# Sample states of a hybrid decoder step: values fetched two steps ahead instead of one

## The chip, the core and the metric

The kernel runs on one core of one Trainium2 chip. The metric is the device time of one execution in microseconds (us); before the change its median is 1824.19 us over three runs.

The engines have these names in the profile: PE is TensorE's matmul, PEld its weight load, DVE is VectorE, ACT is ScalarE, POOL is GpSimd, SP is SyncE. Each engine works through its own queue in order. SP, ACT and POOL also issue DMAs from their queues.

## The reference

One layer of a decoder trunk runs for a prompt of 256 tokens and for 8 samples of one token each. The width is 2048. A combined input projection feeds three parallel mixers: a gated MLP over chunks, HGRN2 (8 heads, 128 x 128 states) and GLA (4 heads, 128 x 256 states). Each mixer's output is projected, gated and summed; an output projection, a residual and a squared-ReLU MLP of width 8192 follow. All weights are float32.

The part that the change touches is the recurrence of the samples. Each sample brings a state per head, and makes one step:

```python
S_t = diag(f_t) S_{t-1} + k_t v_t^T      # per head, dk x dv
o_t = S_t^T q_t
```

The new states are outputs (`hgrn_sample`, `gla_sample`), and `o_t`, normalised per head, goes on into the branch.

## The kernel before

**Matmuls.** Every weight block comes by DMA into a raw buffer (SP's queue, L606 and L613), ACT rounds it into `whi` (L109), DVE takes the rest into `wlo` (L106), and TensorE multiplies three times (L656 to L658): high by high, high by low, low by high. One such block of four 128-row slices by 256 columns is a *granule* of 24 matmuls. Raw buffers and the split tiles `whi` and `wlo` are few, so ACT and DVE run only some granules ahead of TensorE, and SP can load only when a split has emptied a buffer.

**Background work.** After each granule `linear` calls `background()` (L698). It raises the count `now`, pumps two queues of generators, and decides on a *slot*. `bg` holds the mixers of the prompt, `bs` the states of the samples. A queue gains its rate (0.5 per granule for `bs`) and spends 1 at each plain `yield`. A generator that yields a condition is held, without cost, until the condition is true; while held it saves up at most 1. The slot (L665) issues small matmuls for prompt levels (L678) and for samples (L685) that are at least 2 granules old. It comes when a round of the conditioning matrix (`ada`, L376) is due and something waits, or when something has waited for four granules (a GLA sample counts two more).

**Sample states.** `samples_r` (L1066) runs once for each of three groups: HGRN2 heads 0 to 3, HGRN2 heads 4 to 7, and GLA. A step handles one sample for HGRN2 (4 heads, 8 steps) and half a sample for GLA (2 heads, 16 steps). Each step does this:

- `fetch` brings the old states into a tile `st` (L1081), of which there are `ST_BUFS = 4`.
- `values` brings the row of v, broadcast to all partitions, from a DRAM scratch `vs_d` into a tile `vbc` (L1087), of which there are `VB_BUFS = 2`.
- ACT scales the states by the decay (L1107), DVE adds the product of k and v (L1109).
- The new states are stored (L1110), and a whole sample is handed to the slot, whose matmuls (L685) read the same `st` tile. DVE collects their results in `os` (L692, L694).

All four DMAs are issued from POOL's queue. Before step n's computation the generator fetches the states of step n+2 and the values of step n+1. The fetch is held until at most one computed tile is still waiting for its slot (L1100), and the computation until its states were fetched 3 granules ago and its values 2 (L1104).

**What orders the work.** From L972 to L1404 the orders on TensorE and POOL are those of the program text, as written. The orders on ACT, DVE and SP are made by the scheduler, which places each instruction by its own estimate of when the data are there. On the chip an instruction that comes too early in its queue holds up all that stands behind it.

**Who needs the results.** `finish(i)` (L1300) needs the finished `os` of a group: TensorE transposes it (L1307). It is called for both HGRN2 groups at the head of branch 1 and for GLA at the head of branch 2.

**Tiles touched by the change.** `os0`, `os1`, `os2` are three rows of results (128, 128 and 256 columns); the tag `os2` serves again after the output projection as `sp` (L1504). `A1` (L469) holds the scales of the first modulation, `A2` (L1494) those of the second; `G1` (L1407) and `G2` (L1603) hold the gates of the two residuals. Each of these four takes 576 bytes of a partition.

Of the kernel before, what the change touches and what calls it, by code (L numbers as in the profile page):

```python
# [15 lines left out]
P = 128  # L16
D = 2048
KT = D // P
# [3 lines left out]
NC = 1 + NS  # L22
# [13 lines left out]
CHUNKS = (2, 2, 4, 4, 4)  # L36
RATES = ((1.8, 0.5), (1.6, 0.5), (1.25, 0.5), (1.0, 0.5))
ST_BUFS = 4
VB_BUFS = 2
N_PRE = 6  # L40
PRE_AT = (2, 3, 4)
ADA_BATCH = 4
# [15 lines left out]
def hybrid_step_kernel(  # L58
# [8 lines left out]
    nc = tc.nc  # L67
# [14 lines left out]
    def nm(s):  # L82
        uid[0] += 1
        return f"{s}_{uid[0]}"

    def blk(shape=None, dt=F32):
        shape = shape or [P, 4, NT]
        return blkp.tile(shape, dt, tag="b", name=nm("b"))
# [4 lines left out]
    def tmp(shape, tag, bufs=2):  # L93
        return tp.tile(shape, F32, tag=tag, name=nm(tag), bufs=bufs)

    def const(shape, name, dt=F32):
        return cp.tile(shape, dt, tag=name, name=name)

    def mul(o, a, b):
        V.tensor_tensor(o, a, b, op=ALU.mult)  # L100
# [106 lines left out]
    def rstd_small(ms, scale, out):  # L207

        n, w = out.shape
        xx, aa = tmp([P, 16], "sx")[0:n, 0:w], tmp([P, 16], "sa")[0:n, 0:w]  # L210
        c = 0
        for m in ms if isinstance(ms, list) else [ms]:
            V.tensor_scalar(xx[:, c:c + m.shape[1]], m, scale, EPS, ALU.mult, ALU.add)
            c += m.shape[1]
        V.tensor_scalar(out.bitcast(I32), xx.bitcast(I32), -0.5, 1597463007.0, ALU.mult, ALU.add)
        for _ in range(3):
            mul(aa, out, out)
            V.scalar_tensor_tensor(aa, aa, -0.5, xx, ALU.mult, ALU.mult)
            V.scalar_tensor_tensor(out, aa, 1.5, out, ALU.add, ALU.mult)
# [249 lines left out]
    A1 = const([P, KT, NC], "A1")  # L469
# [254 lines left out]
    def tiles(bl):  # L724
        return lambda k: moving(bl[k // 4][:, k % 4, :])
# [123 lines left out]
    def to_tokens(vt):  # L849

        ps = sm()
        for m in range(2):
            for t in range(2):
                T.transpose(ps[:, (2 * m + t) * P:(2 * m + t + 1) * P], vt[:, m, t * P:(t + 1) * P], ident)  # L854
        return ps.rearrange("p (m t f) -> p t m f", m=2, t=2)
# [176 lines left out]
    def gla_group():  # L1032
# [30 lines left out]
        G.gates = gates  # L1063
        return G

    def samples_r(G):  # L1066

        dv = G.dv
        nj, nh = dv // P, 512 // dv
        q, k, g = G.q, G.k, G.g  # L1070
        fs = tmp([P, 4, NS], "fs")
        S.activation(fs, g[:, :, NP:NT], AF.Exp)
        qm = blk([P, 4, NS, 32])
        mul(qm, q[:, :, NP:NT].unsqueeze(3).to_broadcast([P, 4, NS, 32]),
            delta.rearrange("p (b c) -> p b c", b=NS).unsqueeze(1).to_broadcast([P, 4, NS, 32]))
        steps = [(b, h) for b in range(NS) for h in range(0, 4, nh)]
        ahead, vals = [], []

        def fetch(b, h):
            st = tmp([P, nh, dv], "st", ST_BUFS)  # L1080
            nc.gpsimd.dma_start(st, G.s_in(b, h, nh))  # L1081
            ahead.append((st, now[0]))

        def values(b, h):
            v = tmp([P, 4, P], "vbc", VB_BUFS)
            r0 = 4 * nj * b + h * nj
            nc.gpsimd.dma_start(v, vs_d[G.i, r0:r0 + 4, :].partition_broadcast(P))  # L1087
            vals.append((v.rearrange("p (h j) v -> p h (j v)", h=nh), now[0]))

        for s in steps[0:2]:  # L1090
            fetch(*s)
            yield
        values(*steps[0])
        yield
        os_ = tmp([P, dv], f"os{G.i}", 1)
        sts = []
        for n, (b, h0) in enumerate(steps):
            if n + 2 < len(steps):

                yield lambda: len(sts) + sum(len(x[3]) for x in samples) <= ST_BUFS - 3  # L1100
                fetch(*steps[n + 2])
            if n + 1 < len(steps):
                values(*steps[n + 1])
            yield lambda: now[0] >= max(ahead[0][1] + FETCHED, vals[0][1] + FETCHED - 1)  # L1104
            st, v = ahead.pop(0)[0], vals.pop(0)[0]
            for i in range(nh):
                S.activation(st[:, i, :], st[:, i, :], AF.Copy, scale=fs[:, h0 + i, b:b + 1])  # L1107
            for i in range(nh):
                V.scalar_tensor_tensor(st[:, i, :], v[:, i, :], k[:, h0 + i, NP + b:NP + b + 1], st[:, i, :], ALU.mult, ALU.add)  # L1109
            nc.gpsimd.dma_start(G.s_out(b, h0, nh), st)  # L1110
            sts.append(st)
            if h0 + nh == 4:
                samples.append((now[0], (G, qm, os_), b, sts))
                sts = []
            yield
        yield lambda: not samples
        yield READY
        ss, rr = tmp([P, 1], "sss", 1), tmp([P, 1], "srr", 1)
        S.activation(tmp([P, dv], "vt"), os_, AF.Square, accum_out=ss)
        rstd_small(ss, 1.0 / dv, rr)  # L1120
        S.activation(os_, os_, AF.Copy, scale=rr)
        G.os = os_
        yield

    def mixer_r(G):
# [18 lines left out]
        q, k, g = G.q, G.k, G.g  # L1144

        bs.g.append(samples_r(G))


# [258 lines left out]
    G1 = const([P, KT, NC], "G1")  # L1407
# [8 lines left out]
    def gated(m, src, Gv):  # L1416

        k = 2 * m
        sq = tmp([P, 2, NT], "vt")
        g = tmp([P, 2, NT], "gt")  # L1420
        if m < 7:
            S.activation(sq, src, AF.Square)
        else:
            S.activation(sq[:, 0, :], src[:, 0, :], AF.Square)
        V.tensor_scalar(g[:, 1, 0:NP], src[:, 1, 0:NP], Gv[:, k + 1, 0:1], None, ALU.mult)
        if m == 7:
            S.activation(sq[:, 1, :], src[:, 1, :], AF.Square)
        S.activation(g[:, 0, 0:NP], src[:, 0, 0:NP], AF.Copy, scale=Gv[:, k, 0:1])
        if m == 0:
            add(sqacc, sq[:, 0, :], sq[:, 1, :])  # L1430
        else:
            add(sqacc, sqacc, sq[:, 0, :])
            add(sqacc, sqacc, sq[:, 1, :])
        mul(gs[:, k:k + 2, :], src[:, :, NP:NT], Gv[:, k:k + 2, 1:NC])
        return g
# [13 lines left out]
    def put_rows(m, pt, rows):  # L1449
        S.copy(in_rows(rows, 0, m), pt[:, 0])  # L1450
        V.tensor_copy(in_rows(rows, 1, m), pt[:, 1])
# [28 lines left out]
    for m in range(8):  # L1480
        if m in PRE_AT:
            n = N_PRE // len(PRE_AT)
# [8 lines left out]
            S.activation(tmp([P, 1], "srr", 1), sqacc[:, 0:1], AF.Sqrt)  # L1491
    rounds.drain()
    rounds = pre
    A2 = const([P, KT, NC], "A2")  # L1494
    V.scalar_tensor_tensor(A2, mod[:, 4 * KT:5 * KT, :], 1.0, gpre2T.unsqueeze(2).to_broadcast([P, KT, NC]), ALU.add, ALU.mult)
    B2 = mod[:, 3 * KT:4 * KT, :]
    order.__exit__(None, None, None)
# [36 lines left out]
    Q.tensor_tensor(xsT, xsT, gs, op=ALU.add)  # L1534
    Q.tensor_tensor(xa, xsT, A2[:, :, 1:NC], op=ALU.mult)

# [50 lines left out]
    def put_quad(q, i2, i, src, vt):  # L1587
        k = 4 * q + 2 * i2 + i
        if i == 0 and (q == 0 or i2 == 0):
            V.tensor_scalar(vt[:, i, 0:NP], src, A2[:, k, 0:1], B2[:, k, 0:1], ALU.mult, ALU.add)  # L1590
        else:
            S.activation(vt[:, i, 0:NP], src, AF.Identity, scale=A2[:, k, 0:1], bias=B2[:, k, 0:1])
        if q == 0 or i == 1:
# [6 lines left out]

    rate[:] = (0.0, 0.0)
    rounds.pace, rounds.batch = 5, 2
    G2 = const([P, KT, NC], "G2")  # L1603
    h2H, h2L = tiles(h2h), tiles(h2l)

    def begin_up():
# [33 lines left out]
    def down(f, ah, al):  # L1640
        for m in range(8):
# [8 lines left out]
            if f == NFB - 1:  # L1650
                g = gated(m, dst, G2)
                later.append((now[0], lambda m=m, g=g: put_rows(m, to_tokens(g), yt)))
# [6 lines left out]
    for f in range(NFB):  # L1659
        nxt = up(f + 1) if f + 1 < NFB else None  # L1660
        if f == NFB - 1:
            rounds.drain()
            mul(G2, mod[:, 5 * KT:6 * KT, :], gpost2T.unsqueeze(2).to_broadcast([P, KT, NC]))
            yt = [[blk([P, 1024]) for _ in range(2)] for _ in range(2)]
# [23 lines left out]
    def last_tile(i):  # L1688
# [10 lines left out]
        S.activation(sq[:, i, :], d, AF.Square)  # L1699
        V.tensor_scalar(g[:, i, 0:NP], d[:, 0:NP], G2[:, 14 + i, 0:1], None, ALU.mult)  # L1700

# [43 lines left out]

    Q.tensor_tensor(gs[:, 14:16, :], dst[:, :, NP:NT], G2[:, 14:16, 1:NC], op=ALU.mult)  # L1746
    ys = tmp([P, NS, KT], "sqs", 1)
# [61 lines left out]
```

## Time and profile before

| | us |
|---|---|
| median of 3 runs (lowest to highest) | 1824.19 (1822.34 to 1824.85) |
| the profiled execution | 1821.87 |
| its span, first to last instruction | 1820.0 |

| engine | busy us | share of the span |
|---|---|---|
| TensorE | 1780.2 | 98% |
| VectorE | 1178.7 | 65% |
| ScalarE | 996.9 | 55% |
| GpSimd | 136.9 | 8% |

The profile is of one execution. The page lists busy time by engine and by line; other views ask the same trace for the waits (an engine and line, what it waited for, total us, number of times, longest), for stretches of the span, or for the order of time. In the order of time a row has its start, its duration, the engine, the line, the operation, the tiles written and read, and in brackets how long the engine sat idle before it and what ended that. Durations and waits that matter here are quoted with the prediction. GpSimd's DMA rows are only the issue of the transfer; the time to landing is in a table of its own.

### The profile page before, as it was taken

The numbers are of one execution on the slowest core, as the hardware profiler recorded it, in microseconds if no ns is written. First come the engines' busy times: TensorE is split into PE (matmuls) and PEld (weight loads), VectorE is DVE, ScalarE is ACT, GpSimd is POOL, SyncE is SP. The second block draws the span as 40 slices with busy tenths as digits, with TensorE's granted clock in tenths as the row PEclk, the third lists the DMA queues.
The fourth block names the chain that finished last, engine by engine and source line by source line (L and its number), as shares of the span: only waits on it lengthen the run. The fifth ranks groups of instructions, "written<-read, shape, count | busy, mean of one in ns | idle before, by whom it ended". The sixth has DMA issues, their size and how long they took to land.

```text
span 1820.0 us, 42083 instructions
## 1 busy us (share of the span) xinstructions
PE 1780.2 (98%) x16970; PEld 1689.8 (93%) x16970; DVE 1178.7 (65%) x2077; ACT 996.9 (55%) x1824; POOL 136.9 (8%) x228
## 2 busy tenths in 40 slices
PE   6999999999999999999999999999999999999998
PEld 4889999989988989989999989999999999999998
DVE  4666567787577696566555667555666666666666
ACT  5444364676766766654445666555554545454544
POOL 3221000102111111210000000000000000000000
PEclk9999999999999999999999999999999999999999
DMA  9987788788788789897978954777666666666663
GB/s 325 339 348 262 253 282 261 211 257 290 231 290 264 227 271 301 274 321 243 307 248 267 330 168 152 251 256 223 195 196 194 195 196 196 197 196 193 196 193 118
DMA packets 330180, 442.05 MB, mean 243 GB/s; under 512 B 14947, under 2 KB 276945, under 8 KB 329985
## 3 DMA queue, kind: packets, MB, share of 16 engines
q1 hardware_dynamic: 311872, 380.52, 65.1%
q0 software_dynamic: 17184, 57.85, 9.0%
q8 instruction: 133, 2.18, 0.5%
q10 hardware_dynamic: 928, 0.99, 0.2%
q14 instruction: 63, 0.51, 0.1%
HBM read 427.60 MB, written 11.70 MB: 241 GB/s over the span
## 4 chain that ended last, share of the span: by engine, by line
PE 88%; DVE 2%; issue 2%; DMA 1%; ACT 1%; POOL 0%; ACTq 0%; DVEq 0%; POOLq 0%
PE mm L656 27%; PE mm L658 26%; PE mm L657 26%; PE ada L376 3%; DMA vbc<-vs_d 1%; PE ada L308 1%; PE sm L854 1%; DVE wlo L106 1%; PE sm L678 1%; PE sm L685 0%; DVE b L106 0%; PE sm L1578 0%; PE sm L1209 0%; DMA st<-in_state_hgrn_dram 0%; ACT whi L109 0%
## 5 line engine op out<-in xcount | busy, mean ns | idle before, releaser
L656 PE MATMUL mm<-b,whi 128*128 128x264 f32 x4608 | 1286.9, 279 | 6.8 <-ACT whi L109 2.5
L658 PE MATMUL mm<-b,wlo 128*128 128x264 f32 x4608 | 1274.5, 277 | 5.2 <-DVE wlo L106 4.8
L657 PE MATMUL mm<-b,whi 128*128 128x264 f32 x4608 | 1273.4, 276 | 0.5 <-DVE b L106 0.4
L106 DVE TENSOR_TENSOR wlo<-raw,whi 128x512 fp32r<-128x512 f32 x1136 | 768.8, 689 | 443.8 <-ACT whi L109 442.4
L109 ACT CAST whi<-raw 128x512 fp32r<-128x512 f32 x1136 | 688.9, 616 | 626.9 <-DVE wlo L106 310.7
L656 PEld LDWEIGHTS mm<-b,whi 128*128 128x128 f32 x4608 | 872.3, 189 | 48.7 <-issue 26.4
L658 PEld LDWEIGHTS mm<-b,wlo 128*128 128x128 f32 x4608 | 872.3, 189 | 7.1 <-DVE wlo L106 7.1
L657 PEld LDWEIGHTS mm<-b,whi 128*128 128x128 f32 x4608 | 872.4, 189 | 1.1 <-DVE b L106 0.6
L103 DVE TENSOR_TENSOR b<-b,mm 128x528 f32<-128x528 f32 (+1 forms) x137 | 95.4, 698 | 63.3 <-PE mm L658 55.6
L1109 DVE SCALAR_TENSOR_TENSOR st<-vbc,b,st 128x128 f32<-128x128 f32 (+1 forms) x96 | 34.2, 392 | 52.4 <-DMA vbc<-vs_d 45.9
L1107 ACT ACTIVATE st<-st,fs 128x128 f32<-128x128 f32 (+1 forms) x96 | 37.0, 430 | 48.2 <-DMA st<-in_state_hgrn_dram 28.2
L1746 POOL TENSOR_TENSOR gs<-b,G 128x16 f32<-128x16 f32 x1 | 0.2, 222 | 714.1 <-DVE b L103 714.1
L485 POOL DMA_DIRECT2D b<-in_w_ada_dram x64 | 46.3, 725 | 48.0 <-PE ada L308 30.4
L376 PE MATMUL ada<-araw,cT 128*32 128x512 f32 x296 | 40.7, 601 | 0.0
L308 PE MATMUL ada<-b,cT 128*32 128x256 f32 (+1 forms) x640 | 35.0, 355 | 5.3 <-DMA b<-in_w_ada_dram 5.3
L100 DVE TENSOR_TENSOR b<-b,b 128x512 f32<-128x512 f32 (+1 forms) x47 | 34.0, 743 | 1.3 <-ACT b L1221 1.0
L308 PEld LDWEIGHTS ada<-b,cT 128*32 128x32 f32 x640 | 17.8, 113 | 17.4 <-DMA b<-in_w_ada_dram 9.6
L1110 POOL DMA_DIRECT2D out_dram<-st x32 | 23.5, 735 | 129.5 <-DVE st L1109 129.5
L376 PE MATMUL ada<-b,cT 128*32 128x512 f32 x216 | 26.2, 593 | 0.0
L106 DVE TENSOR_TENSOR b<-gt,b 128x528 fp32r<-128x528 f32 x32 | 22.7, 711 | 3.2
L106 DVE TENSOR_TENSOR b<-b,b 128x1056 fp32r<-128x1056 f32 (+3 forms) x21 | 20.9, 993 | 5.9 <-ACT b L109 5.9
L106 DVE TENSOR_TENSOR b<-b 128x1024 f32<-128x1024 f32 (+1 forms) x24 | 24.3, 1018 | 0.0
(360 smaller groups left out, 895.8 us busy)
## 6 DMA issues: line engine op xcount, KB each, us to landing
raw<-in_w_in_dram SPq DMA_DIRECT2D x231, 512.0 KB, 5.0
raw<-in_w_mlp_up_dram SPq DMA_DIRECT2D x128, 512.0 KB, 3.9
raw<-in_w_mlp_down_dram SPq DMA_DIRECT2D x128, 512.0 KB, 3.7
araw<-in_w_ada_dram SPq DMA_DIRECT2D x74, 512.0 KB, 5.7
b<-in_w_ada_dram SPq DMA_DIRECT2D x54, 512.0 KB, 6.4
b<-in_w_ada_dram POOLq DMA_DIRECT2D x48, 512.0 KB, 11.3
raw<-in_w_branch_dram SPq DMA_DIRECT2D x48, 512.0 KB, 4.6
raw<-in_w_out_dram SPq DMA_DIRECT2D x32, 512.0 KB, 5.1
```

Of the source, the lines that this page charges most:

```text
L100: V.tensor_tensor(o, a, b, op=ALU.mult)
L103: V.tensor_tensor(o, a, b, op=ALU.add)
L106: V.tensor_tensor(o, a, b, op=ALU.subtract)
L109: S.copy(hi, src)
L308: T.matmul(acc[32 * j:32 * j + 32, 0:n], cT[:, k, :], w[:, n * j:n * j + n], start=k == 0, stop=k == KT - 1)
L376: T.matmul(self.acc[32 * j:32 * j + 32, :], cT[:, k, :], ws[j // 2][:, j % 2 * 512:j % 2 * 512 + 512], start=k == 0, stop=k == KT - 1)
L485: queue.dma_start(w[:, i], w1[k * P:(k + 1) * P, :, self.k0 * P:(self.k0 + self.n) * P])
L656: T.matmul(o, a, xh(k + j), start=first and j == 0, stop=False)
L657: T.matmul(o, a, xl(k + j), start=False, stop=False)
L658: T.matmul(o, b, xh(k + j), start=False, stop=last and j == n - 1)
L1107: S.activation(st[:, i, :], st[:, i, :], AF.Copy, scale=fs[:, h0 + i, b:b + 1])
L1109: V.scalar_tensor_tensor(st[:, i, :], v[:, i, :], k[:, h0 + i, NP + b:NP + b + 1], st[:, i, :], ALU.mult, ALU.add)
```

## The change

Three things change in `samples_r`. The values of the first two steps are asked for before the loop, with one more `yield`. In the loop, the values of step n+2 are asked for first, then the store of the step before is issued, and then, behind the held condition, the states of step n+2 are fetched; a step's own store is only put aside, and the last one is issued after the loop. `vbc` has three buffers.

Room for the third buffer (2 KB of each partition) comes from tiles: the two HGRN2 groups share one row of results with the tag `os2`, which GLA then takes anew, `A2` is the tile of `A1`, and `G2` that of `G1`.

```diff
-VB_BUFS = 2
+VB_BUFS = 3
...
+    os_rows = []
+
     def samples_r(G):
...
         for s in steps[0:2]:
             fetch(*s)
             yield
-        values(*steps[0])
-        yield
-        os_ = tmp([P, dv], f"os{G.i}", 1)
-        sts = []
+        for s in steps[0:2]:
+            values(*s)
+            yield
+        if G.i != 1:
+            os_rows.append(tmp([P, 256], "os2", 1))
+        os_ = os_rows[-1][:, G.i % 2 * P:G.i % 2 * P + dv]
+        sts, out = [], []
         for n, (b, h0) in enumerate(steps):
             if n + 2 < len(steps):
+                values(*steps[n + 2])
+            if out:
+                nc.gpsimd.dma_start(*out.pop())
+            if n + 2 < len(steps):
 
                 yield lambda: len(sts) + sum(len(x[3]) for x in samples) <= ST_BUFS - 3
                 fetch(*steps[n + 2])
-            if n + 1 < len(steps):
-                values(*steps[n + 1])
             yield lambda: now[0] >= max(ahead[0][1] + FETCHED, vals[0][1] + FETCHED - 1)
...
-            nc.gpsimd.dma_start(G.s_out(b, h0, nh), st)
+            out.append((G.s_out(b, h0, nh), st))
             sts.append(st)
...
             yield
+        nc.gpsimd.dma_start(*out.pop())
         yield lambda: not samples
...
-    A2 = const([P, KT, NC], "A2")
+    A2 = A1
...
-    G2 = const([P, KT, NC], "G2")
+    G2 = G1
```

## The prediction, before the change was run

> **What bounds the kernel now.** I read the page first, then stretches of the span, then the waits by stage, then the order of time at two places. The page has TensorE busy for nearly the whole span, so a change can only win what TensorE idles, or what it loses to a lower clock.
>
> ```profile
> PE 1780.2 (98%) x16970; PEld 1689.8 (93%) x16970; DVE 1178.7 (65%) x2077; ACT 996.9 (55%) x1824; POOL 136.9 (8%) x228
> ```
>
> The table of stretches (length, then busy time and instructions of PE, PEld, DVE, ACT, POOL, then clock, DMA share, GB/s) says where that idle time lies.
>
> ```profile
> 350.00:500.00 150.00, 147.22 (x1650) 137.02 (x1649) 109.72 (x211) 110.64 (x225) 21.97 (x34) 0.99 0.79 252
> 500.00:630.00 130.00, 126.89 (x1489) 117.74 (x1489) 91.02 (x183) 87.23 (x191) 13.74 (x20) 1.00 0.81 264
> 630.00:810.00 180.00, 174.97 (x1852) 162.28 (x1852) 125.64 (x220) 107.55 (x218) 34.55 (x52) 0.99 0.87 290
> 1120.00:1800.00 680.00, 680.00 (x6036) 672.19 (x6035) 423.32 (x646) 352.55 (x585) 0.00 (x0) 1.00 0.67 203
> ```
>
> The first three are the stretches in which the samples' states of the three groups are done (two HGRN2 groups, then GLA). TensorE idles 2.78, 3.11 and 5.03 us in them, 10.9 us together. The last row, the MLP, idles nothing and no edit reaches into it. The waits of TensorE alone, in the same three stretches, name the stalls (total, times, longest):
>
> ```profile
> PE mm L656 <- ACT whi L109: 1.8, 1, 1.8
> PE mm L658 <- DVE wlo L106: 1.0, 2, 0.6
> ...
> PE mm L656 <- ACT att L1187: 1.3, 1, 1.3
> PE mm L658 <- DVE wlo L106: 0.8, 2, 0.4
> PE sm L678 <- issue: 0.6, 1, 0.6
> ...
> PE mm L658 <- DVE wlo L106: 2.8, 1, 2.8
> PE sm L678 <- issue: 2.2, 1, 2.2
> ```
>
> TensorE is stopped by weights that ACT and DVE have not split yet. These two run their queues in order, and the waits of the whole span say what holds them up:
>
> ```profile
> DVE st L1109 <- DMA vbc<-vs_d: 45.9, 18, 7.2
> ACT st L1107 <- DMA st<-in_state_hgrn_dram: 28.2, 9, 8.9
> ACT st L1107 <- DMA st<-in_state_gla_dram: 13.7, 8, 2.8
> ```
>
> Behind a waiting L1109 on DVE stand splits (L106), and for the splits wait TensorE and the loads into the raw buffers. The change aims at the first row. The second and third rows, the states themselves, are the same kind of wait on ACT.
>
> **The order on the GpSimd queue.** Write F(n) for the fetch of step n's states (L1081), V(n) for its values (L1087), C(n) for its two computations (L1107, L1109), S(n) for the store (L1110). Before, the queue reads F(n+1), V(n), S(n-1), F(n+2), V(n+1), S(n). After, it reads F(n+1), V(n+2), S(n-1), F(n+2), V(n+3), S(n). So V(n+2) stands where V(n) stood, and all F and S keep their order. V(n+2) needs the buffer that C(n-1) read last, of three; the store S(n-1) behind it waits for the same C(n-1). The new wait on GpSimd therefore holds nobody longer than the store did: F(n+2) and what follows are issued as before. Cost 0; the store's wait is the cover, and without it the cost would be one DVE group, 0.9 us (the 0.88 us of L1109 in the next rows). Numbers of instructions and DMAs are unchanged: 32 of each kind.
>
> **What it is worth, place by place.** First the end of the GLA group:
>
> ```profile
> 782.21 0.72 POOL L1081 DMA_DIRECT2D st<-in_state_gla_dram  x1
> 788.41 0.71 POOL L1110 DMA_DIRECT2D out_dram<-st  x1 [4.91 <-DVE st L1109]
> 789.12 0.58 POOL L1087 DMA_DIRECT2D vbc<-vs_d  x1
> 789.69 0.51 ACT L1107 ACTIVATE st<-st,fs 128x256 f32<-128x256 f32 x1
> 795.95 0.88 DVE L1109 SCALAR_TENSOR_TENSOR st<-vbc,b,st 128x256 f32<-128x256 f32 x2 [4.25 <-issue]
> 796.74 4.38 DVE L106 TENSOR_TENSOR wlo<-raw,whi 128x512 fp32r<-128x512 f32 x7
> ```
>
> The last values went out at 789.12, only after the store of step 13, though the states of step 15 had been fetched at 782.21 and scaled at 789.69. DVE stood 4.25 us for them with seven splits queued behind; TensorE ran dry and lost the 2.78 us of the waits above. After the change V(15) goes out before S(12) and F(15), so it is there before its states: DVE's 4.25 us exceed TensorE's 2.78 us, and I take the whole stall away. A stall this long also costs clock:
>
> ```profile
> 398.00:400.00 2.00, 1.56 (x8) 1.50 (x8) 1.97 (x5) 2.00 (x4) 0.00 (x0) 0.56 0.19 26
> 400.00:402.00 2.00, 2.00 (x12) 2.00 (x12) 2.00 (x4) 1.65 (x4) 0.00 (x0) 0.59 1.01 328
> 674.00:676.00 2.00, 2.00 (x21) 2.00 (x20) 2.00 (x6) 1.88 (x4) 0.00 (x0) 1.00 0.93 312
> 798.00:800.00 2.00, 2.00 (x11) 2.00 (x11) 2.00 (x5) 1.02 (x3) 0.00 (x0) 0.50 0.75 194
> 800.00:802.00 2.00, 2.00 (x16) 1.85 (x19) 1.19 (x3) 0.58 (x2) 0.00 (x0) 0.75 1.01 302
> ```
>
> From 798 to 802 us the clock was 0.50 and 0.75: (0.50 + 0.25) x 2 us = 1.5 us of work lost. So the end is worth **2.8 + 1.5 = 4.3 us** (bounds 0 and 4.3). The Trainium skill ("TensorE: Matmul & The Clock Gate", Part 1: The HAM clock gate) says that after an idle window of about 3.4 us the clock halves, and needs as long of work to return. By that rule, 1.7 us a stall, the end is worth 4.5 us. The trace agrees here (0.50), but shows that not each stall pays: after the one of 2.2 us at 672 us the clock was 1.00 in the next row.
>
> Second, the starts of the two HGRN2 groups. The first:
>
> ```profile
> 388.30 0.76 POOL L1110 DMA_DIRECT2D out_dram<-st  x1 [28.22 <-DVE st L1109]
> 389.05 0.75 POOL L1081 DMA_DIRECT2D st<-in_state_hgrn_dram  x1
> 389.80 0.55 POOL L1087 DMA_DIRECT2D vbc<-vs_d  x1
> 396.03 0.98 ACT L1107 ACTIVATE st<-st,fs 128x128 f32<-128x128 f32 x3 [8.91 <-DMA st<-in_state_hgrn_dram]
> 396.97 0.88 DVE L1109 SCALAR_TENSOR_TENSOR st<-vbc,b,st 128x128 f32<-128x128 f32 x3 [6.11 <-DMA vbc<-vs_d]
> ```
>
> S(0) released F(3) and V(2) one after the other. V(2) goes out at the start of the group after the change, but F(3) still stands behind S(0), and ACT still waits for it: the wait moves from the values to the states, 0.94 us earlier at most (396.97 less 396.03). TensorE lost 1.75 + 0.43 us here, the 1.8 by ACT and part of the 1.0 by DVE, and (0.44 + 0.41) x 2 = 1.7 us of clock, which on the 1.56 us busy of the first row makes 1.5. I take the DVE part, **0.4 us** (bounds 0 and 2.2 + 1.5 = 3.7). The second group's start is of the same kind with 0.8 us of DVE splits in the waits: I take **0.8 us** (0 to 0.8). The remaining stalls, 1.3 us by ACT's `att` and 2.8 us of "issue", have no value transfer as releaser: 0 (bounds 0 and 4.1).
>
> Third, the many short waits in between: DVE will now follow L1107 directly, so what it saves is the time by which values landed after states. TensorE did not stop there; 0.
>
> **The other parts.** The extra yield in front of each group shifts C(0) by two granules (a granule is one background call, 24 matmuls, about 680 us x 24 / 6036 = 2.7 us in the MLP's row). With two steps' values in hand the gate on values never holds, and both steps of a GLA sample come in one granule. Counting the pump's rules by hand, the last slot comes at granule 53 instead of 49 for the first group, at 93 for the second as before, at 142 instead of 148 for GLA. The outputs are asked for at 98, 98 and 162, so nobody waits: 0. If the second group slipped past 98, TensorE would wait for L1119 to L1121, some 4 us by these rows, which is no part of my sum:
>
> ```profile
> 616.66 0.31 ACT L1119 ACTIVATE vt<-os 128x128 f32<-128x128 f32 x1
> 620.09 0.40 ACT L1121 ACTIVATE os<-os,srr 128x128 f32<-128x128 f32 x1 [0.85 <-DVE srr L219]
> ```
>
> The shared tiles add only write-after-read waits. `A2` over `A1` waits for the modulation, over since the input projection; `G2` over `G1` waits for the last gated tile of the output projection, six MLP blocks earlier; the GLA row over the HGRN2 row waits for transposes that stand three granules ahead of that group's start. All are long past: 0, and if one were not, one small DVE operation late, below the 0.9 us named. The GpSimd queue also carries the prompt states' stores (L1254); their place among the samples' entries shifts by a step at most, which I price at 0.
>
> **Sum**, against the profiled execution (1821.87 us, span 1820.0): 4.3 + 0.4 + 0.8 = 5.5 us, so 1816.4 us. That execution lies 2.3 us below the median 1824.19 of the runs shown, so on the median's scale **1818.7 us**.
>
> **Rivals.**
>
> *The wait only changes its transfer.* ACT's 28.2 + 13.7 us for states stay, DVE follows ACT, and the last steps stop on F(14) and F(15) as they stopped on V(15). For it: F(n) keeps its place, and the two kinds land alike (rows below). Against it: F(15) had landed by 789.69, six us before V(15). What is left is the 0.4 and 0.8 us: 1.2 us, 1823.0.
>
> *GLA crowds the DMA engines (slower).* By the count above a GLA sample takes 4 granules instead of 5 or 6. It moves two steps of F, V and S, six transfers:
>
> ```profile
> vbc<-vs_d POOLq DMA_DIRECT2D x32, 256.0 KB, 6.3
> out_dram<-st POOLq DMA_DIRECT2D x32, 256.0 KB, 5.5
> st<-in_state_gla_dram POOLq DMA_DIRECT2D x16, 256.0 KB, 5.8
> 700.00:720.00 20.00, 20.00 (x188) 19.35 (x184) 11.78 (x21) 11.77 (x23) 3.98 (x6) 1.00 1.00 340
> 780.00:800.00 20.00, 17.22 (x142) 16.32 (x135) 11.08 (x21) 9.64 (x19) 6.00 (x9) 0.94 0.98 362
> ```
>
> That is 6 x 0.26 = 1.57 MB, in 4 x 2.7 = 10.8 us 145 GB/s instead of some 106 at 5.5 granules; 39 GB/s more on the 290 of the stage's row is 329, next to the 340 to 362 at which the DMA share reads 1.00 and 0.98. The point from which it decides: a share of 1.0 through several slots, so that raw weights land late and ACT's splits wait for them. Each such stall costs what the end of GLA cost, 4.3 us. With three of them, 12.9 - 5.5 = 7.4 us slower: 1831.6. Against it: 700 to 720 had a share of 1.00 and no idle TensorE. The Trainium skill ("DMA: Bandwidth & Descriptors", SWDGE vs HWDGE vs iDMA) says that inside a DMA engine the GpSimd's queue and the hardware queues take turns, so samples' transfers would take time from weights; no row here shows the turns themselves.
>
> *The start goes too.* If the planner, which orders DVE and ACT anew, puts L1107 of step 3 behind some splits, the first start's other 3.3 us (3.7 - 0.4) go as well: 1815.4.
>
> **Chances.** Forecast 0.42; the wait moves 0.20; crowding 0.30; the start too 0.08. A difference of 0.2%, 3.6 us, is about what a measurement can tell from none. The forecast counts as faster but for 0.02; the wait that moves counts as the same for 0.18, the rest as either side. Faster 0.48, same 0.20, slower 0.32. The forecast's own range is 1815 to 1821; the range for 8 in 10 reaches to the start's full gain with part of the 4.1 us that I left at 0 (1815.4 - 3.4 = 1812) and to crowding with three stalls (1831).
>
> **What would show it.** Right: no wait for `vbc` over 1 us in the DVE waits, TensorE's 2.8 us stall near the end of GLA gone, the clock 1.0 there, ACT's waits for `st` near 42 us as before. Wrong: DVE waits of 4 us or more at L1109, now for ACT or `st`; TensorE stalls in the GLA stage with a DMA share of 1.0 and ACT waiting for `raw`; a wait at L1307. The forecast falls if TensorE idles over 9 us from 350 to 810 us.

## The result, and the profile after

| | median us | runs | ratio to before |
|---|---|---|---|
| before, run beside it | 1821.84 | 6 | |
| after | 1829.38 (1827.42 to 1831.76) | 6 | 1.0036 [1.0023, 1.0049] |

The changed kernel is **slower by 0.36%, 6.6 us** (4.2 to 8.9 by the interval). The profiled execution has a span of 1827.4 us, where before's had 1820.0.

First the same stretches of the span as before, in the changed kernel, with the same columns (length, busy time of PE, PEld, DVE, ACT, POOL, then clock, DMA share, GB/s).

```profile
350.00:500.00 150.00, 147.22 (x1660) 137.43 (x1659) 108.73 (x207) 110.69 (x226) 21.18 (x34) 1.00 0.78 252
500.00:630.00 130.00, 128.22 (x1501) 118.40 (x1500) 94.43 (x191) 89.99 (x194) 14.43 (x22) 1.00 0.82 268
630.00:810.00 180.00, 169.72 (x1796) 156.12 (x1795) 124.30 (x223) 105.88 (x217) 34.50 (x52) 0.98 0.85 282
```

TensorE idles 2.78, 1.78 and 10.28 us, where it idled 2.78, 3.11 and 5.03 us. The HGRN2 groups are a little better, the GLA group is much worse, and the DMA share in the GLA stretch has not risen (0.85, before 0.87). The starts of the same TensorE groups in both traces give the lag of the changed kernel along the span (start before, lag after; worked out from the two traces):

```
at  92 us  -0.4      at 408 us  +1.9      at 833 us  +7.4
at 124 us  +2.6      at 568 us  +0.7      at 1259 us +7.4
at 373 us  +3.3      at 650 us  +0.9
```

So three things add up to 7.4 us in these two executions: 3.3 us are lost **before the first edited instruction** (the values that POOL asks for at 361.50 us); 2.4 us are won in the HGRN2 stages; 6.5 us are lost in the GLA stage.

The waits of TensorE in the GLA stage (640 to 815 us) of the changed kernel (what was waited for: total, times, longest), and then the waits of DVE and ScalarE over its whole span:

```profile
PE mm L656 <- ACT gt L1348: 5.0, 1, 5.0
PE sm L1257 <- ACT b L1260: 2.8, 1, 2.8
PE mm L658 <- DVE wlo L106: 1.2, 2, 0.8
```

```profile
DVE st L1116 <- ACT st L1114: 37.6, 20, 4.9
ACT whi L109 <- DMA raw<-in_w_in_dram: 32.8, 18, 3.4
ACT st L1114 <- DMA st<-in_state_hgrn_dram: 29.7, 9, 8.8
ACT st L1114 <- DMA st<-in_state_gla_dram: 27.4, 10, 7.0
```

DVE's 45.9 us for `vbc` are gone, as is TensorE's 2.8 us for `wlo`. In their place DVE waits 37.6 us for ScalarE's scaling, ScalarE waits 27.4 us for GLA's states (13.7 before), and TensorE has a stall of 5.0 us behind it. ScalarE's wait for raw weights is no longer than before (32.8 us; 34.5 in the row below, of the kernel before).

```profile
ACT whi L109 <- DMA raw<-in_w_in_dram: 34.5, 18, 4.0
```

In order of time, the place of the 5.0 us, with POOL's, ScalarE's and TensorE's rows of the changed kernel:

```profile
665.88 0.56 POOL L1089 DMA_DIRECT2D vbc<-vs_d  x1 [26.20 <-DVE st L1116]
666.42 0.72 POOL L1106 DMA_DIRECT2D out_dram<-st  x1
667.14 0.73 POOL L1083 DMA_DIRECT2D st<-in_state_gla_dram  x1
...
675.98 0.91 ACT L1114 ACTIVATE st<-st,fs 128x256 f32<-128x256 f32 x2 [6.96 <-DMA st<-in_state_gla_dram]
676.80 0.60 ACT L109 CAST whi<-raw 128x512 fp32r<-128x512 f32 x1
677.30 0.60 ACT L1348 ACTIVATE gt<-mm 128x528 f32<-128x528 f32 x1
...
677.96 0.59 PE L656 MATMUL mm<-b,whi 128*128 128x264 f32 x1 [5.05 <-ACT gt L1348]
```

The same place in the kernel before, with V(2) (L1087) behind F(3) (L1081):

```profile
662.23 0.71 POOL L1110 DMA_DIRECT2D out_dram<-st  x1 [25.08 <-DVE st L1109]
662.93 0.72 POOL L1081 DMA_DIRECT2D st<-in_state_gla_dram  x1
663.65 0.57 POOL L1087 DMA_DIRECT2D vbc<-vs_d  x1
...
669.03 0.91 ACT L1107 ACTIVATE st<-st,fs 128x256 f32<-128x256 f32 x2 [2.74 <-DMA st<-in_state_gla_dram]
```

The rows of the changed kernel are one chain: V(3), S(0) and F(3) all leave POOL once C(0) is done; ScalarE has come to the scaling of step 3, stands 6.96 us until F(3) has landed 8.8 us after its issue, and a split and the copy `gt`, which TensorE needs, stand behind it. ScalarE came there 1.9 us after F(3) was issued (675.98 less 6.96 less 667.14), in the kernel before 3.4 us after (669.03 less 2.74 less 662.93). So of the 4.2 us that its wait grew, 1.5 us are a later issue and 2.7 us a later landing. Issue to landing of F(3), with the transfers around it, from 655 to 676 us, first of the kernel before, then of the changed one:

```profile
out_dram<-st POOLq DMA_DIRECT2D x2, 256.0 KB, 5.5
st<-in_state_gla_dram POOLq DMA_DIRECT2D x1, 256.0 KB, 6.0
vbc<-vs_d POOLq DMA_DIRECT2D x1, 256.0 KB, 7.1
```

```profile
vbc<-vs_d POOLq DMA_DIRECT2D x2, 256.0 KB, 6.1
out_dram<-st POOLq DMA_DIRECT2D x2, 256.0 KB, 6.3
st<-in_state_gla_dram POOLq DMA_DIRECT2D x1, 256.0 KB, 8.8
```

With the values behind it the states took 6.0 us; with the values ahead of it, 8.8 us. In the profiles of the experiments below, F(3) took 6.0 to 6.5 us in all twelve further runs that issue no values just ahead of it, and 7.2 to 8.7 us in the five that issue V(3) there. (In fetch_first2_aligned it is issued long before its place here.) The clock rows of the changed kernel show what the stall cost besides, and that the end of GLA and the start of the HGRN2 group no longer cost clock (the rows from 402 to 412 and from 800 to 808 us show 1.00 too):

```profile
400.00:402.00 2.00, 0.69 (x6) 0.49 (x5) 1.64 (x6) 2.00 (x6) 0.00 (x0) 1.00 1.08 397
676.00:678.00 2.00, 0.04 (x1) 0.05 (x1) 0.57 (x1) 2.00 (x5) 0.00 (x0) 0.50 0.42 152
678.00:680.00 2.00, 2.00 (x9) 2.00 (x10) 2.00 (x5) 1.50 (x3) 0.00 (x0) 0.50 0.37 103
680.00:682.00 2.00, 2.00 (x11) 2.00 (x10) 2.00 (x6) 1.24 (x3) 0.00 (x0) 0.50 0.82 268
798.00:800.00 2.00, 2.00 (x22) 1.46 (x21) 2.00 (x4) 1.24 (x2) 0.00 (x0) 1.00 1.05 397
```

Two rows at half clock with TensorE busy are 2 us of work, so this one place costs about 7 us. The kernel before had a stall of 2.2 us near it, at L678, without a lower clock after it; that one is gone here.

### The profile page after: what moved, and what is told of

Same layout as the page of the kernel before. It is cut to its first block, busy times and chain, and to the rows that moved or that the text cites. A ratio compares the mean times of both kernels' runs of the same rounds, so it can differ in the third digit from the quotient of the medians.

```text
span 1827.4 us, 42084 instructions
## 1 busy us (share of the span) xinstructions
PE 1783.8 (98%) x16970; PEld 1691.2 (93%) x16970; DVE 1182.6 (65%) x2076; ACT 997.5 (55%) x1824; POOL 136.7 (7%) x228
## 4 chain that ended last, share of the span: by engine, by line
PE 83%; issue 4%; DMA 3%; DVE 2%; ACT 2%; POOL 1%; SPq 0%; ACTq 0%; DVEq 0%; POOLq 0%
PE mm L656 25%; PE mm L658 25%; PE mm L657 25%; PE ada L376 3%; DMA st<-in_state_gla_dram 2%; PE ada L308 1%; DVE wlo L106 1%; DMA st<-in_state_hgrn_dram 1%; ACT whi L109 1%; DVE b L106 1%; PE sm L854 1%; PE sm L678 0%; PE sm L685 0%; DMA araw<-in_w_ada_dram 0%; PE sm L1586 0%
## 5 line engine op out<-in xcount | busy, mean ns | idle before, releaser
L1114 ACT ACTIVATE st<-st,fs 128x128 f32<-128x128 f32 (+1 forms) x96 | 37.0, 430 | 63.5 <-DMA st<-in_state_hgrn_dram 29.7
L1116 DVE SCALAR_TENSOR_TENSOR st<-vbc,b,st 128x128 f32<-128x128 f32 (+1 forms) x96 | 34.4, 396 | 44.8 <-ACT st L1114 37.6
L1640 ACT ACTIVATE b<-vt 128x528 fp32r<-128x528 f32 x32 | 22.9, 714 | 1.0
```

## The experiments

Ratios are to the kernel before on the same chip, with a 95% interval; 0.001 is 1.8 us. All kernels have the same matrix products.

### Is it the room or the loop?

`room_only` is the kernel before with the shared tiles alone (old loop, two buffers); the orders on every engine are those of the kernel before.

```diff
+        if G.i != 1:
+            os_rows.append(tmp([P, 256], "os2", 1))
-        os_ = tmp([P, dv], f"os{G.i}", 1)
+        os_ = os_rows[-1][:, G.i % 2 * P:G.i % 2 * P + dv]
...
-    A2 = const([P, KT, NC], "A2")
+    A2 = A1
...
-    G2 = const([P, KT, NC], "G2")
+    G2 = G1
```

> The edits that make room alone (shared row of results, A2 on A1, G2 on G1), with the old loop and two value buffers; the orders on all engines are those of before. Theory (the loss lies in the GLA stage, where ACT waits for states fetched after the first store): no difference, within 2 us of before. Rival (the tiles' new places cost something: the changed kernel was 3.2 us later already at the first store of values, before any edited order): 2 to 4 us slower than before, with the loss ahead of 350 us.

Measured: 1827.08 us, ratio **1.0021 [1.001, 1.0032]**. The edits that the prediction priced at nothing cost 3.8 us: the theory of this run missed, and its rival came true.

`new_hgrn` has the change with the new loop for the HGRN2 groups only, `new_gla` with the new loop for GLA only. The old order is kept where `new` is false (in new_gla `new` is `G.i == 2`):

```diff
+        new = G.i < 2
+        for s in steps[0:2] if new else steps[0:1]:
+            values(*s)
+            yield
...
+            if new and n + 2 < len(steps):
+                values(*steps[n + 2])
...
+            if not new and n + 1 < len(steps):
                 values(*steps[n + 1])
...
```

> The new loop for the two HGRN2 groups only; GLA keeps the old loop (three value buffers for all). Theory: the changed kernel gained 2.3 us between 350 and 634 us, so 1 to 3 us faster than before; GLA's stall of 5.0 us at its start is gone. Rival (new places of the tiles): 1 to 3 us slower than before.

> The new loop for GLA only; the HGRN2 groups keep the old one. Theory: the changed kernel lost 6.5 us between 634 and 850 us, so 5 to 8 us slower than before, with TensorE stalls behind ACT's wait for st near the start of GLA. Rival (new places of the tiles, or the HGRN2 groups): within 3 us of before.

Measured: new_hgrn 1824.78 us, **1.0003 [0.9993, 1.0013]**; new_gla 1829.68 us, **1.0036 [1.002, 1.0053]**. Against room_only on the same chip the new loop is worth -3.3 us in HGRN2 and +2.7 us in GLA (differences of the ratios). new_hgrn was not faster than the kernel before, as its theory had it. new_gla is as slow as the whole change (1.0036), so the two loops' prices don't simply add.

`same_start` is the change without the extra yield in front of each group.

```diff
         for s in steps[0:2]:
             values(*s)
-            yield
+        yield
```

> The changed kernel without its extra yield: the values of steps 0 and 1 are asked for in one go, so each group's first computation comes at the same granule as before. Theory (two granules later, F(3) behind the first store falls due late and ACT waits 7 us for it): the 5.0 us stall at the start of GLA goes, and the time is within 3 us of before, 1820 to 1825. Rival (GLA's samples at 4 granules each crowd the DMA engines, whatever the start): stays 5 us or more slower than before.

Measured: 1826.47 us, **1.0017 [1.0006, 1.0028]**, 3.5 us below the change. TensorE's stall for `gt` was 2.5 us here, half of the change's 5.0 us; the theory had it gone.

### What of the room?

`before_again` is the kernel before, unedited. `os_only` shares the row of results alone, `a2g2_only` the two pairs of constants alone; `room_padded` shares everything, and unused tiles of the same size fill the room.

```diff
-    A2 = const([P, KT, NC], "A2")
+    const([P, KT, NC], "A2")
+    A2 = A1
...
```

> The kernel before, unchanged, as a yardstick: no difference in time; what its second profile shows at 90 to 104 us. If the lower clock there (0.5 for some 6 us in every other profile, 1.00 in the first profile of before) belongs to the tiles' places, the clock is 1.00 again; if it falls by chance, it may be 0.5 here too.

> Only the shared row of results; the large tiles (weights, splits) keep the addresses of before. Theory (the loss of 3.8 us comes from moving the weight and split tiles by 1152 bytes, off a multiple of 1024): no difference from before, within 1.5 us. Rival (the shared row itself): 2 to 4 us slower.

> Only A2 on A1 and G2 on G1, which moves all large tiles down by 1152 bytes. Theory (tiles' places): the whole loss, 2 to 5 us slower than before. Rival (the shared row, or the aliases only where they are used): no difference.

> All three edits that make room, but the room filled with unused tiles, so that weights, splits and all large tiles lie where they lay before. Theory (tiles' places): no difference from before, within 1.5 us, while room_only lost 3.8 us. Rival (the aliases make a wait): 2 to 5 us slower, as room_only.

| kernel | shares | large tiles moved by | us | ratio |
|---|---|---|---|---|
| before_again | nothing | 0 | 1821.97 | 1.0003 [0.9992, 1.0014] |
| os_only | row of results | 0 | 1822.14 | 0.9997 [0.9987, 1.0007] |
| a2g2_only | A2, G2 | 1152 bytes | 1827.54 | 1.0014 [1.0004, 1.0025] |
| room_padded | all | 0 | 1823.03 | 0.9999 [0.999, 1.0009] |

Sharing costs nothing where nothing moves. `A2` and `G2` lie ahead of the blocks, the raw and the split weights in each partition; without them all of those lie 1152 bytes lower (the blocks begin at byte 33664, not 34816).

`after_aligned` and `a2g2_aligned` are the change and a2g2_only with one unused tile of 128 bytes there, so that the large tiles lie 1024 bytes lower than before.

```diff
+    const([P, 32], "pad")
```

> The changed kernel with an unused tile of 128 bytes per partition ahead of the large tiles, so that the blocks begin at byte 33792 (33 x 1024) and not at 33664; the raw and split weights too move up by 128 bytes, to 1024 bytes below their old place. Theory (it is the place within 1024 bytes that cost a2g2_only and room_only 3 to 4 us, while the loop's new order costs its own 3 to 4 us in the GLA group): about 3 us off the changed kernel's 1829.4, 1826.5 us, a ratio to the kernel before of 1.0015 to 1.0025, with TensorE's stalls for ACT near 677 and 734 us still there. Rival (any other place costs it, or the blame on the place is wrong): 1829.4, a ratio of 1.0036.

> The kernel before with A2 = A1 and G2 = G1 alone, and the same unused 128 bytes: the large tiles lie 1024 bytes lower than in the kernel before, where a2g2_only had them 1152 lower. Theory (the place within 1024 bytes decides): as the kernel before, ratio 0.999 to 1.001, 2.5 us faster than a2g2_only's 1827.5 (ratio 1.0014). Rival (the distance moved decides, whatever its remainder): ratio 1.0014 again.

Measured: after_aligned 1826.28 us, **1.0022 [1.0007, 1.0036]**; a2g2_aligned 1822.74 us, **1.0000 [0.9988, 1.0012]**. In both pairs 128 bytes take back 0.0014, 2.6 us, but in both the two intervals overlap. With two runs of the next section there are five pairs of kernels that differ in nothing but the place of these tiles:

| 1152 bytes lower | not moved, or 1024 bytes lower | difference of the ratios |
|---|---|---|
| room_only | room_padded | 0.0022 |
| a2g2_only | a2g2_aligned | 0.0014 |
| the change | after_aligned | 0.0014 |
| new_hgrn | new_hgrn_aligned | 0.0012 |
| same_start | same_start_aligned | -0.0001 |

Only the first pair is clear of noise by itself, and the last shows nothing. The mean is 0.0012, 2.2 us, with an uncertainty of about 0.0008 (an estimate from the ten intervals).

Part of it shows at the start of the kernel, in the stretch from 92 to 104 us, first a2g2_only, then a2g2_aligned:

```profile
92.00:104.00 12.00, 9.24 (x63) 7.80 (x60) 3.68 (x7) 1.61 (x3) 0.00 (x0) 0.72 0.62 227
```

```profile
92.00:104.00 12.00, 9.68 (x89) 8.60 (x90) 6.31 (x13) 4.92 (x9) 2.74 (x7) 1.00 0.60 218
```

A clock of 0.72 over 12 us is at most 3.4 us of work; the lag of the changed kernel grew by 3.0 us between 92 and 124 us. Over all 20 profiles: of the six kernels with the large tiles 1152 bytes lower, five had 0.72 there and one 0.86; of the 14 others seven had 1.00, six 0.86, one 0.72. So the clock is lost there by chance (v_behind and v_behind_again are one kernel, with 1.00 and 0.86), and the place shifts the odds.

### What of the GLA loop?

`new_hgrn_aligned` is new_hgrn with the 128 bytes. `fetch_first2_aligned` is after_aligned with the fetch in front of values and store in the loop:

```diff
             if n + 2 < len(steps):
-                values(*steps[n + 2])
-            if out:
-                nc.gpsimd.dma_start(*out.pop())
-            if n + 2 < len(steps):
 
                 yield lambda: len(sts) + sum(len(x[3]) for x in samples) <= ST_BUFS - 3
                 fetch(*steps[n + 2])
+                values(*steps[n + 2])
+            if out:
+                nc.gpsimd.dma_start(*out.pop())
```

> The new loop for the two HGRN2 groups alone, the old loop for GLA, with the shared tiles, three buffers and the unused 128 bytes. Theory: the HGRN2 stages keep their gain of 2.3 us, nothing is lost to the place or in GLA: 2 to 3 us off new_hgrn's 1824.8, 1821.5 to 1822.5, a ratio of 0.9985 to 0.9995, faster than the kernel before. Rival (the places don't matter to it, or the gain there is given back later in the kernel): ratio 1.000 to 1.001.

> after_aligned with one thing changed in the loop: the states of step n+2 are fetched first, then its values, then the store of the step before; so the fetch stands behind neither the values that wait for a buffer nor the store. The extra yield stays. Theory (in GLA the fetch of step 3 was issued late, because values and store ahead of it on the GpSimd queue wait for the first step's computation; ScalarE then stood 7 us for those states with TensorE's splits behind it): TensorE's 5.0 us stall near 677 us and most of ScalarE's 27 us of waits for GLA's states go, 3 to 5 us faster than after_aligned: 1822 to 1823.5, a ratio of 0.999 to 1.0005. Rival (the states land late because the DMA engines are full there, whenever they are asked for): the stall stays, within 1 us of after_aligned.

Measured: new_hgrn_aligned 1821.11 us, **0.9991 [0.9981, 1.0002]**; so after_aligned's GLA loop costs 0.0031, 5.6 us. fetch_first2_aligned 1846.21 us, **1.0136 [1.0117, 1.0155]**: a plain miss, some 21 us on the wrong side of the theory. One place of its POOL queue and the waits of DVE show how time was lost:

```profile
672.17 0.72 POOL L1110 DMA_DIRECT2D out_dram<-st  x1
689.68 0.73 POOL L1084 DMA_DIRECT2D st<-in_state_gla_dram  x1 [16.79 <-PE sm L685]
690.40 0.57 POOL L1090 DMA_DIRECT2D vbc<-vs_d  x1
690.96 0.71 POOL L1110 DMA_DIRECT2D out_dram<-st  x1
```

```profile
DVE st L1116 <- DMA vbc<-vs_d: 73.2, 16, 9.0
```

The fetch of step 4 waits 16.8 us until TensorE has read the first sample out of its buffer, and now values and store wait with it. TensorE's stall for `gt` is gone here, as the theory had it, but this run changed three orders at once, so it can't price the one at 667 us.

`same_start_aligned` is same_start with the 128 bytes. `v_behind` differs from it in the order on POOL: store of step n-1, fetch of n+2, and the values of n+2 last. (The scheduler also moved one split on ScalarE and two on VectorE by a few rows.) `v_behind_gla` has the change's loop for HGRN2 and v_behind's for GLA.

```diff
-            if n + 2 < len(steps):
-                values(*steps[n + 2])
             if out:
                 nc.gpsimd.dma_start(*out.pop())
             if n + 2 < len(steps):
 
                 yield lambda: len(sts) + sum(len(x[3]) for x in samples) <= ST_BUFS - 3
                 fetch(*steps[n + 2])
+                values(*steps[n + 2])
```

> after_aligned without the extra yield: the loop of each group begins one background call earlier, as in the kernel before. Theory (the yield puts the first computation of a GLA step, and with it the fetch of step 3 that stands behind it on the GpSimd queue, two background calls later, while ScalarE's place for that step stays): 2.5 to 3 us off after_aligned, ratio 1.0005 to 1.001; the stall near 677 us falls below 3 us. Rival (the order on the GpSimd queue alone makes GLA slower): ratio 1.002 as after_aligned.

> Values two steps ahead as in the change, but put behind the fetch: store of step n-1, fetch of step n+2, values of step n+2; no extra yield, three buffers, the large tiles on a multiple of 1024. No store and no fetch stands behind values that wait for a buffer. Theory (values ahead are worth what the prediction said, at GLA's end above all; what they cost is the late store and fetch, and the places): the kernel before less 3 to 5 us, ratio 0.997 to 0.9985, no TensorE stall over 3 us from 640 to 850 us. Rival (DMA order is not it; any order in which values come earlier moves ScalarE's waits for GLA's states): ratio 1.0005 to 1.002.

> The change's loop for the two HGRN2 groups (extra yield too), v_behind's for GLA, the large tiles on a multiple of 1024: new_hgrn_aligned with another GLA loop. Theory: new_hgrn_aligned's 0.9991 less GLA's end, 2 to 4 us: ratio 0.997 to 0.998. Rival: GLA is crowded by any earlier values, ratio 1.000 or more.

Measured: same_start_aligned 1827.0 us, **1.0018 [1.001, 1.0027]**; v_behind 1821.19 us, **0.9990 [0.9979, 1.0002]**; v_behind_gla 1821.97 us, **0.9993 [0.9985, 1.0002]**. The place of the values in the queue is worth 0.0028, 5.1 us. The extra yield, worth 3.5 us between the change and same_start, is worth 0.7 us here, with overlapping intervals: what it costs stays open, and the expectation for same_start_aligned was missed. v_behind was expected 3 to 5 us under the kernel before and came 1.8 us under it; v_behind_gla missed its 0.997 to 0.998.

`one_front` is v_behind with three rows on POOL exchanged and no other row on any engine: at GLA's step 1 the values of step 3 go ahead of the store of step 0 and the fetch of step 3. `one_behind` has the values in front everywhere but there (`front` negated).

```diff
+            front = G.i == 2 and n == 1
+            if front and n + 2 < len(steps):
+                values(*steps[n + 2])
             if out:
                 nc.gpsimd.dma_start(*out.pop())
...
                 fetch(*steps[n + 2])
-                values(*steps[n + 2])
+                if not front:
+                    values(*steps[n + 2])
```

> v_behind with three rows of the GpSimd queue in another order and nothing else, on any engine: at GLA's third fetch the queue has values of step 3, store of step 0, states of step 3, where v_behind has store, states, values. Theory (transfers of the GpSimd queue follow each other, so a 256 KB transfer issued just ahead of the states makes them land later, with ScalarE, and behind it TensorE's splits, waiting): the states of step 3 land 8 to 9 us after their issue instead of v_behind's 6.2; ScalarE waits 5 to 6 us for them instead of 2.9; TensorE's stall by gt near 670 us, absent in v_behind, is back with 2 to 4 us: 2 to 4 us slower than v_behind, ratio 1.000 to 1.0015. Rival (it is the density of the whole stage, not this place): within 1 us of v_behind.

> same_start_aligned with those three rows alone in v_behind's order (store of step 0, states of step 3, values of step 3), all other steps with the values in front. Theory: the stall by gt near 676 us (2.0) and part of the clock lost there go, 2 to 3 us faster than same_start_aligned, a ratio of 1.000 to 1.001; what is left of its distance to v_behind comes from later steps. Rival: as same_start_aligned, 1.0018.

> The same kernel as v_behind, to compare one_front with on the same chip: 0.999 again, 0.998 to 1.000.

Measured: one_front 1824.89 us, **1.0008 [0.9999, 1.0017]**; one_behind 1823.89 us, **1.0004 [0.9996, 1.0013]**; v_behind_again 1820.35 us, **0.9982 [0.9971, 0.9993]**. By the medians three rows cost 4.5 us (ratios 0.0026 apart, and the intervals don't overlap), and putting them back in the other kernel wins 2.6 us. Landing of F(3), from the table from 655 to 676 us, in one_front and in v_behind_again:

```profile
st<-in_state_gla_dram POOLq DMA_DIRECT2D x1, 256.0 KB, 8.5
```

```profile
st<-in_state_gla_dram POOLq DMA_DIRECT2D x1, 256.0 KB, 6.1
```

The scaling of step 3 in order of time, in the same two:

```profile
672.47 0.91 ACT L1118 ACTIVATE st<-st,fs 128x256 f32<-128x256 f32 x2 [5.76 <-DMA st<-in_state_gla_dram]
```

```profile
668.61 0.91 ACT L1114 ACTIVATE st<-st,fs 128x256 f32<-128x256 f32 x2 [2.83 <-DMA st<-in_state_gla_dram]
```

And TensorE's waits from 640 to 815 us, again one_front first:

```profile
PE mm L656 <- ACT gt L1352: 2.3, 1, 2.3
PE sm L678 <- issue: 2.1, 1, 2.1
PE sm L685 <- ACT b L1246: 1.4, 1, 1.4
PE sm L1306 <- ACT b L1297: 0.5, 1, 0.5
```

```profile
PE sm L678 <- issue: 2.8, 1, 2.8
PE sm L685 <- ACT b L1242: 1.7, 1, 1.7
PE sm L1302 <- ACT b L1293: 1.2, 2, 0.7
PE mm L658 <- DVE wlo L106: 0.5, 2, 0.3
```

A transfer of 256 KB issued just ahead makes the states land 2.4 us later, ScalarE waits 2.9 us longer, and TensorE has the stall by `gt`, which v_behind does not have. How much of that lasts is less sure. By the starts of the same TensorE groups in these two executions one_front is 1.0 us behind at 650 us, 5.0 at 690 us and 2.9 from 833 us on: the place costs 4.0 us, of which 2.1 us are made up later. TensorE's idle time over the stage is nearly equal (6.5 and 6.4 us between 630 and 810 us), because one_front's other stalls are shorter. What differs is the clock between 660 and 690 us, one_front first:

```profile
660.00:690.00 30.00, 25.52 (x497) 23.85 (x500) 24.69 (x45) 14.43 (x28) 6.68 (x10) 0.89 0.71 217
660.00:690.00 30.00, 27.22 (x529) 24.74 (x530) 26.60 (x47) 16.37 (x32) 6.69 (x10) 1.00 0.82 263
```

So what the three rows cost lastingly is in part clock, which the last section shows to fall differently in two executions of one kernel.

**The best version** is v_behind: 0.9990 and 0.9982 in two sets of runs, about 0.1 to 0.2% faster than the kernel before; the interval of the first set still holds no difference.

## Why the prediction was wrong

The forecast was 1818.7 us and faster; the result is slower. That it lies inside the wide range (1812 to 1831) is luck: that end of the range was kept for crowding, which is not what happened. Two steps failed, both priced at nothing, and a third, also priced at nothing, had a part.

**"The new wait on GpSimd therefore holds nobody longer than the store did: F(n+2) and what follows are issued as before. Cost 0."** What releases the queue was read rightly: in the trace the one wait of 26.20 us, at V(3), released V(3), S(0) and F(3) together. But F(3) was not issued as before: V(3)'s own issue, 0.56 us, now stands ahead of it. And to count only issue and wait was too little. A transfer moved ahead also goes through the DMA engines ahead. F(3) landed 8.8 us after its issue instead of 6.0, and it is what ScalarE's in-order queue was waiting for. one_front against v_behind_again shows this by three rows: 4.5 us by the medians, 1.9 us of which the two traces show as lasting. In the chain of ratios GLA's loop costs 5.6 us in all (after_aligned less new_hgrn_aligned); how the rest divides between the later steps and the extra yield is not settled.

**The extra yield: "so nobody waits: 0."** The prediction asked only whether the outputs would be late. In the three profiles with the yield and the values ahead (the change, after_aligned, new_gla) ScalarE reaches the scaling of step 3 1.9 us after F(3)'s issue; in three with the values ahead and no yield (same_start, same_start_aligned, one_front) it is 2.8 to 2.9 us, so with the yield F(3) goes out some 0.9 us later for ScalarE. And TensorE's second stall of the waits above, 2.8 us at L1257 behind scalings of states, stands in those three at 2.8 to 3.6 us, in fetch_first2_aligned, which has the yield too, at 4.2 us, and in no other kernel. What the yield costs in all, 3.5 us or 0.7 us by the two pairs of runs, stays open.

**"The shared tiles add only write-after-read waits ... All are long past: 0."** The waits were indeed nothing (os_only and room_padded, 0.9997 and 0.9999). But less room in front moved every large tile, and that cost 4.0 us between room_only and room_padded, 2.2 us in the mean of the five pairs, and nothing in one of them. The prediction had no term for where tiles lie. The Trainium skill ("DMA: Bandwidth & Descriptors", How a descriptor splits into AXI transactions) states that the first transaction of a descriptor that does not start on a multiple of 256 bytes starts at the 256-byte boundary below, and that the bytes before the start are fetched but unused and still cost beats, the steps in which the bus moves data. The page speaks of bytes that are fetched; here the weights' tiles are what the transfers fill. The blocks began at byte 34816 before, at 33664 after and at 33792 with the 128 bytes; the first and the last are multiples of 256, the second is not. The sign agrees with the runs, but the traces hardly show the mechanism: the median landing of the 512 KB of `raw<-in_w_in_dram` was 5.0 to 5.3 us in the six kernels that lie 1152 bytes lower, and 4.8 to 5.1 us in the 14 others. Only moves by 0, 1024 and 1152 bytes were run, so which remainder matters stays open, as does by what path it reaches the clock at 92 to 104 us.

The terms of the sum themselves:

- *End of GLA, 4.3 us.* Right at its place: the stall of 2.8 us and the half clock are gone (clock 1.00 at 798 us). But it is no gain of the GLA group. Even in v_behind_again, which keeps it, stalls of 1.7 and 1.2 us at L685 and L1302, for ScalarE, came instead, ahead of that place (between 720 and 780 us), and v_behind_gla (0.9993) is no faster than new_hgrn_aligned (0.9991), whose GLA loop is the old one. The prediction did not say what is late next.
- *Starts of the HGRN2 groups, 0.4 + 0.8 us.* Undersized. The lag falls by 2.4 us; TensorE's idle time fell by nothing in the first stage and by 1.33 us in the second, and the rest agrees with the clock: 1.00 in the rows from 400 to 412 us, where it was 0.59 at 400 us. The prediction had the 1.5 us of clock among its bounds but left it out. As it said, ScalarE's wait for HGRN2's states stayed (29.7 us, 28.2 before).
- *Short waits in between, 0.* DVE's 45.9 us for `vbc` became 37.6 us for ScalarE, as foreseen, and no gain of it shows.

**The rivals.** "GLA crowds the DMA engines" gave 1831.6 us, 2.2 us from the result, but not for its reason: the DMA share of the stage fell from 0.87 to 0.85 and ScalarE's wait for raw weights from 34.5 to 32.8 us. What the runs show instead is one transfer ahead of another in one queue, not a higher load of the stage. Of "the wait only changes its transfer" the first half came true, and its worst case was missing: the wait did not only stay with the states, it doubled, from 13.7 to 27.4 us. Of the signs named in advance, waits of over 4 us at DVE's line for ScalarE (4.9 us) and over 9 us of idle TensorE between 350 and 810 us (2.78 + 1.78 + 10.28 = 14.8 us) both came.

The change's ratio as a chain: place 0.0014 (change less after_aligned), GLA's loop 0.0031 (after_aligned less new_hgrn_aligned), HGRN2's loop -0.0009 (new_hgrn_aligned less 1) make 0.0036, as they must by the way they are taken. Each has an uncertainty of about 0.001 to 0.002. Without the 128 bytes HGRN2's loop was worth -0.0018 beside GLA's old loop (new_hgrn less room_only) and nothing beside GLA's new one (the change less new_gla).

## What to carry to other kernels

When a DMA is moved ahead in a queue, price not only what it waits for but also what its transfer pushes back: ask which transfer behind it an in-order engine is waiting for, and put the less urgent one behind that. A change that frees or adds a small tile moves all tiles laid out after it; keep their places with an unused tile, and measure the layout by itself before a small difference is put down to the rest of the edit. And a stall removed in a chain of in-order queues is worth something only once it is known what is late next.

## What the runs showed of the hardware that was not expected

- Weight tiles that lay 1152 bytes lower cost 2.2 us of 1822 in the mean of five pairs of kernels (4.0 us to nothing); at 1024 bytes lower, three of four pairs won 2.2 to 2.6 us back.
- A 256 KB transfer issued on GpSimd's queue 1.3 us ahead of another delayed its landing from 6.1 to 8.5 us, with no other instruction of the kernel in another place. In 19 of the 20 profiles the states of step 3 landed after 7.2 to 8.8 us with the values just ahead of them (six) and after 6.0 to 6.5 us without (13).
- The same stall need not cost the same clock. v_behind and v_behind_again are one kernel, and in both TensorE stopped 2.78 us near 670 us. The row after it, first of v_behind, then of v_behind_again:

```profile
672.00:674.00 2.00, 2.00 (x11) 2.00 (x10) 2.00 (x5) 1.38 (x3) 0.00 (x0) 0.50 0.86 289
```

```profile
672.00:674.00 2.00, 2.00 (x20) 2.00 (x19) 2.00 (x5) 0.15 (x2) 0.00 (x0) 1.00 1.00 361
```

Half clock in one, full clock in the other; so a term for clock is a chance and not a fixed price. The Trainium skill ("TensorE: Matmul & The Clock Gate", Part 1: The HAM clock gate) says that the window of some 3.4 us runs free of the kernel, so that the moment of a change depends on where in it the work falls; these two rows agree with that.
